# A decoder block with product-key experts: V rows beside the second search scaled by ScalarE and added by GpSimd, head norms' powers taken per projection, U tiles, rows and the spill's issue moved

## The chip, the core and the metric

The kernel runs on one core of a Trainium2 chip. The metric is the time of one execution on the device in microseconds. The engines are called by the profile's names: PE (TensorE; PEld is its weight load), DVE (VectorE), ACT (ScalarE), POOL (GpSimd) and SP (SyncE, which here only issues transfers). Each engine works through its own instructions in a fixed order; an instruction that waits holds up all those behind it on its engine.

## What is computed

One layer of a decoder block on 512 tokens of width 1024, all in f32. First come three token mixers (attention with forget gates, attention in a window, attention to 256 memory tokens) that are merged and added to x. Then comes a layer of 16384 experts, each a single neuron with a row of `u` and a row of `v`; every token picks 128 of them through two sets of 128 keys:

```python
h = rmsnorm(x, norm1_g); z = h @ w_in                    # q, k, v of the mixers, gate logits
fq = head_rmsnorm(fq, fox_q_g); fk = head_rmsnorm(fk, fox_k_g)    # likewise sq, sk, mq, mk
x += (gates0 * (o_fox @ w_fox_o) + gates1 * (o_swa @ w_swa_o) + gates2 * (o_mem @ w_mem_o)) @ w_out
h = rmsnorm(x, norm2_g); q = h @ w_q                     # 8 heads of 2 halves of 128
v1, i1 = top_k(q[..., 0] @ keys1, 16); v2, i2 = top_k(q[..., 1] @ keys2, 16)
sv, si = top_k(v1[:, None] + v2[None, :], 16)            # of 256 sums, per head
experts = i1[si // 16] * 128 + i2[si % 16]; g = softmax(sv)
x += sum_e gelu(h . u[experts_e]) * g_e * v[experts_e]   # 8 * 16 experts per token
```

## The kernel before

The 512 tokens are four blocks of 128, in two groups: block 0, and blocks 1, 2 and 3. Products of weights with activations are made of three matmuls (`mm3`, L129) from a rounded high part `whi` and the rest `wlo`: ACT rounds each loaded piece (L107), and DVE (L119) or POOL (L117) subtracts. `share[0]` says which part of the subtractions goes to POOL.

The experts are done in two ways. For blocks 0 and 1 the chosen rows of `u` and `v` are fetched one by one: a row job (`step`, L812) fetches, for one of the 128 choices, the 128 tokens' rows with one indirect transfer issued by POOL (L821, 128x1024 f32), and DVE either multiplies and sums it (a U row, L831) or adds it, scaled, to the result (a V row, L837). There are 512 such jobs in a fixed order: 128 U rows and 128 V rows of block 0, then the same of block 1. For blocks 2 and 3 all experts are computed: for each of 128 groups of experts a U tile (`dense_u`, L898: 8 matmuls of `uT` with the tokens, then a gelu on ACT, L918), and later a V tile (`dense_v`, L1027), with the gates of all experts written to DRAM in between ("spill").

Times from the trace's start, in stages:

- 0 to 198 us: mixers of block 0.
- 198 to 690 us: mixers of blocks 1 to 3 (`mixers(1, hT)`, L885). Beside them runs `beside()` (L839): first the search of block 0, then `choose`, then row jobs. `pump` (L69) hands out this side work: each load of weights adds `PACE` of the current kind to a credit, and each piece of side work takes its cost from it. Row jobs are made at a lower priority (`LATER`), so the scheduler may place them later than they stand in the program.
- 690 to 846 us: the second search (L925 to L936), for blocks 1 to 3. PE makes the scores of 8 heads (two `gemm_tr` each, L707, L711), ACT copies them out (L714), DVE finds the top 16 of each half and of the pairs (`top16`, L669), and POOL adds the pairs' sums `cand` (L686). `FIRST_U` = 8 U tiles stand in between.
- 846 to 906 us: `COVER` U tiles on PE, beside the gate weights (`weigh`, L734: three exponentials on ACT between two table loads, L741) and `choose` on DVE; then `BETWEEN` row jobs. From here on (L940) POOL, DVE and PE keep the order of the program; ACT and SP are placed by the scheduler.
- 906 to 1045 us: the spread: 64 batches of 4 tokens. DVE makes one-hot matrices (L967), POOL (odd batches, L970) or ACT (even ones, L973) scale them by the gate, PE multiplies (L985), ACT copies out (L988), and SP issues the spill every fourth batch (L991). `DURING` U tiles and 0.7 row jobs per batch stand between.
- 1045 to 1769 us: `AFTER` U tiles, then for each of 128 groups the gates are loaded back (L1006) and multiplied (L1023, L1020), and the V tile follows, with the remaining U tiles and row jobs spread evenly.

`LAG`, the U tiles that stand ahead of the first V tile, is `FIRST_U + COVER + DURING + AFTER` = 55. The tag `mm` has two PSUM banks (L61), so PE can be two U tiles ahead of ACT's gelus. Names: `tp`, `sc`, `mm`, `acc`, `tg` are PSUM banks; `two` and `raw` are loaded tiles of weights, `row` a fetched row tile, `mg` the sum x (block 0's is the first).

## Time and profile before

| | |
|---|---|
| median of 3 runs | 1769.74 us (1764.91 to 1773.3) |
| the profiled execution | 1770.86 us, of which the span of the trace is 1769.0 us |
| PE busy | 1617.1 us (91% of the span) |
| DVE, POOL, ACT busy | 1367.1, 871.8, 674.5 us (77%, 49%, 38%) |
| granted TensorE clock, mean | 0.96 |
| bytes moved | 540.16 MB, mean 305 GB/s |

PE is busy nearly throughout, but a busy share says only that an instruction is in flight, and it is a mean over stages with different limits. So the stages are read one by one; the granted clock is a share of the full 2.4 GHz, and 0.5 is the lower level of 1.2 GHz.

### The profile page before, as it was taken

What the parts mean: (1) busy time and instruction counts of PE and PEld (TensorE: products, weight loads), DVE (VectorE), ACT (ScalarE), POOL (GpSimd) and SP (SyncE); (2) the same over time, 40 slices, a digit from 0 to 9 for tenths busy, and PEclk for the clock granted to TensorE, in tenths of its full rate; (3) what the DMA queues carried; (4) which work ended last, traced back from release to release, by engine and by line L of the source; (5) the groups of instructions that cost most, each with busy time, mean ns of one, the idle gap of its engine ahead of it and who ended that gap; (6) DMA issues with size and microseconds to landing.
All of it is one profiled execution on the core that took longest, in us unless ns stands there. A gap on an engine that the chain in (4) does not pass through costs nothing.

```text
span 1769.0 us, 25245 instructions
## 1 busy us (share of the span) xinstructions
PE 1617.1 (91%) x8718; PEld 1383.7 (78%) x8718; DVE 1367.1 (77%) x2593; ACT 674.5 (38%) x1488; POOL 871.8 (49%) x728
## 2 busy tenths in 40 slices
PE   6998788998998989798799989999999999998987
PEld 6998687896987978787689978777777767776765
DVE  4777557878989999999989946766767667777767
ACT  6876555555344434221136632222222222222221
POOL 0100375546555558984058843544545445454542
PEclk8999898998998999899899999999999999999999
DMA  6887455878998998785489998999999999999986
GB/s 256 258 242 221 131 167 193 318 269 284 321 332 290 317 332 299 244 291 201 143 320 371 401 390 314 394 347 368 354 375 348 367 360 366 377 380 354 371 324 224
DMA packets 218255, 540.16 MB, mean 305 GB/s; under 512 B 18448, under 2 KB 96528, under 8 KB 218128
## 3 DMA queue, kind: packets, MB, share of 16 engines
q1 hardware_dynamic: 144400, 270.09, 43.3%
q0 software_dynamic: 73728, 268.47, 41.9%
q8 instruction: 68, 1.11, 0.3%
q14 instruction: 59, 0.48, 0.1%
HBM read 519.61 MB, written 18.87 MB: 304 GB/s over the span
## 4 chain that ended last, share of the span: by engine, by line
PE 32%; issue 31%; POOL 15%; DVE 10%; DMA 9%; ACT 3%; SPq 0%; POOLq 0%; DVEq 0%; ACTq 0%
POOL row L821 13%; PE mm L914 6%; PE mm L131 5%; PE mm L133 5%; PE mm L132 5%; DMA row<-in_peer_v_dram,eidx 5%; DVE mg L837 3%; DMA row<-in_peer_u_dram,eidx 3%; PE sc L985 1%; PE tp L985 1%; DVE wlo L119 1%; DVE tmp L673 1%; ACT whi L107 1%; PE sc L486 1%; PE tp L339 1%
## 5 line engine op out<-in xcount | busy, mean ns | idle before, releaser
L821 POOL DMA_INDIRECT row<-in_peer_u_dram,eidx x256 | 320.8, 1253 | 331.4 <-DVE scr L831 264.6
L821 POOL DMA_INDIRECT row<-in_peer_v_dram,eidx x256 | 333.9, 1304 | 281.1 <-DVE mg L837 218.5
L914 PE MATMUL mm<-h2f,two 128*128 128x256 f32 x1920 | 444.0, 383 | 16.3 <-ACT ga L918 10.1
L914 PEld LDWEIGHTS mm<-h2f,two 128*128 128x128 f32 x1920 | 364.4, 193 | 76.5 <-issue 14.6
L107 ACT CAST whi<-raw 128x1024 fp32r<-128x1024 f32 (+1 forms) x268 | 280.2, 1049 | 354.5 <-DMA raw<-in_peer_v_dram 170.5
L119 DVE TENSOR_TENSOR wlo<-raw,whi 128x1024 fp32r<-128x1024 f32 (+1 forms) x233 | 285.3, 1226 | 156.2 <-ACT whi L107 154.4
L837 DVE SCALAR_TENSOR_TENSOR mg<-row,acts,mg 128x1024 f32<-128x1024 f32 x256 | 356.6, 1393 | 19.1 <-DMA row<-in_peer_v_dram,eidx 16.1
L831 DVE SCALAR_TENSOR_TENSOR scr<-row,h2n 128x1024 bf16<-128x1024 f32 x256 | 314.0, 1227 | 19.9 <-DMA row<-in_peer_u_dram,eidx 12.9
L131 PE MATMUL mm<-whi,hhi 128*128 128x256 f32 (+1 forms) x576 | 167.1, 292 | 6.7 <-ACT hhi L623 1.9
L132 PE MATMUL mm<-wlo,hhi 128*128 128x256 f32 (+1 forms) x576 | 167.1, 291 | 2.2 <-DVE wlo L119 2.2
L133 PE MATMUL mm<-whi,hlo 128*128 128x256 f32 (+1 forms) x576 | 165.9, 290 | 1.8 <-DVE hlo L624 1.2
L918 ACT ACTIVATE ga<-mm 128x256 f32<-128x256 f32 x128 | 49.0, 385 | 285.8 <-PE mm L914 279.2
L131 PE MATMUL sc<-whi,ah 128*128 128x512 f32 x192 | 93.4, 486 | 39.8 <-ACT ah L126 39.8
L131 PE MATMUL mm<-hhi,whi 128*128 128x384 f32 x320 | 112.4, 351 | 8.8 <-ACT qp L707 5.6
L117 POOL TENSOR_TENSOR wlo<-raw,whi 128x1024 fp32r<-128x1024 f32 (+1 forms) x35 | 83.8, 2402 | 71.8 <-ACT whi L107 71.6
L131 PEld LDWEIGHTS mm<-whi,hhi 128*128 128x128 f32 x576 | 110.8, 193 | 10.1 <-ACT hhi L623 2.2
L133 PE MATMUL mm<-hhi,wlo 128*128 128x384 f32 x320 | 111.8, 349 | 4.2 <-POOL wlo L117 4.2
L132 PEld LDWEIGHTS mm<-wlo,hhi 128*128 128x128 f32 x576 | 111.3, 193 | 5.2 <-DVE wlo L119 3.1
L133 PEld LDWEIGHTS mm<-whi,hlo 128*128 128x128 f32 x576 | 110.9, 193 | 4.0 <-DVE hlo L624 1.4
L132 PE MATMUL mm<-hlo,whi 128*128 128x384 f32 x320 | 111.3, 348 | 1.5 <-DVE hlo L215 1.5
L179 POOL TENSOR_TENSOR rsy<-rsv,mhalf 128x4 f32<-128x4 f32 (+7 forms) x17 | 38.4, 2265 | 138.6 <-DVE rsv L178 138.4
L127 DVE TENSOR_TENSOR al<-gq,ah 128x256 fp32r<-128x256 f32 x96 | 40.8, 425 | 80.2 <-ACT ah L126 78.5
(260 smaller groups left out, 3020.5 us busy)
## 6 DMA issues: line engine op xcount, KB each, us to landing
raw<-in_peer_v_dram SPq DMA_DIRECT2D x128, 512.0 KB
two<-in_uT_dram SPq DMA_DIRECT2D x60, 1024.0 KB
raw<-in_w_nat_dram SPq DMA_DIRECT2D x40, 512.0 KB
gd<-st SPq DMA_DIRECT2D x32, 512.0 KB
gq<-gd SPq DMA_DIRECT2D x120, 128.0 KB
raw<-in_w_tr_dram SPq DMA_DIRECT2D x48, 256.0 KB
raw<-in_w_o_dram SPq DMA_DIRECT2D x24, 512.0 KB
raw<-in_w_tr_dram SPq DMA_DIRECT2D x24, 512.0 KB
```

Source lines behind the costliest of these rows:

```text
L107: A.copy(hi[:, :n * w], raw[:, :n * w])
L117: G.tensor_tensor(lo, raw, hi.bitcast(F32), op=OP.subtract)
L119: V.tensor_sub(lo, raw, hi.bitcast(F32))
L127: V.tensor_sub(lo, src, hi.bitcast(F32))
L131: PE.matmul(ps, lh, rh, start=first, stop=False)
L132: PE.matmul(ps, lh, rl, start=False, stop=False)
L133: PE.matmul(ps, ll, rh, start=False, stop=last)
L821: G.indirect_dma_start(out=r, out_offset=None, in_=t["peer_" + tab], in_offset=bass.IndirectOffsetOnAxis(ap=eidx[b][:, j:j + 1], axis=0))
L831: V.scalar_tensor_tensor(scr, r, 1.0, h2n[b], op0=OP.mult, op1=OP.mult, accum_out=acts[b][:, c]))
L837: V.scalar_tensor_tensor(x1[b], r, acts[b][:, c], x1[b], op0=OP.mult, op1=OP.add))
L914: PE.matmul(ps[:, :TD], w[:, dc], h2f[dc], start=dc == 0, stop=dc == KC - 1)
L918: A.activation(ga[k], ps[:, :TD], AF.Gelu)
```

## The change

It does six things. (1) During the second search a V row of block 0 is not scaled and added by one DVE instruction but scaled by ACT and added by POOL (`step(apart=True)`), a job for each 2.8 units of search cost; `beside()` ends at 176 jobs. The low parts `wlo` of that search go to DVE (`share[0]` 0.0, before 1.0). (2) The sums of pairs are made for the three blocks by one POOL instruction, right behind a head's top 16. (3) The search and `choose` of block 0 run at a higher pace, and fewer of the low parts beside them go to POOL (0.5 and 0.0, before 0.9 and 0.35). (4) The powers of the head norms, on POOL, are taken per projection, not for key and query (or two projections) together. (5) Three U tiles move from ahead of the spread into it, and two from behind it into it; the gate weights stand behind 14 covering tiles, before 5; two more row jobs stand ahead of the spread. (6) In the spread one batch in four is scaled by POOL, before one in two; the spill is issued by ACT, before by SP.

```diff
-FIRST_U, COVER, DURING, AFTER = 8, 20, 20, 7
-BETWEEN, UNWEIGHED, IN_RAW = 10, 5, 0
+FIRST_U, COVER, DURING, AFTER = 8, 17, 25, 5
+BETWEEN, UNWEIGHED, IN_RAW = 12, 14, 0
-PACE = {"search": 6.0, "choose": 4.0, "rows": 3.5}
+PACE = {"search": 9.0, "choose": 8.0, "rows": 3.5}
+EARLY_ROWS, PER_ROW = 176, 2.8
...
-    class Heads:
...
-        def scale(self):
-            r = rsqrt_mean(self.ss[:, :self.cols], self.cols, self.parts[0][3])
...
+    def heads(lhs, src, nb, nh, hd, pad=0, n=None, also=None):
...
+        ss = small_f(BIG * 4, "hss")[:, :nb * nh]
...
+        gemm_nat(lhs, src, n or nh * hd, nb, use)
+        r = rsqrt_mean(ss, nb * nh, hd)
+        for b in range(nb):
...
+            for h in range(nh):
+                A.activation(z[:, b, h, :hd], z[:, b, h, :hd], AF.Copy, scale=r[:, b * nh + h:b * nh + h + 1])
...
+        def candidates(v12):
+            cand = qq.tile([128, nb, NC], F32, tag="cand", name="cand")
+            for i0, ni, nj, c0 in ROWS:
+                G.tensor_tensor(cand[:, :, c0:c0 + ni * nj].rearrange("p b (i j) -> p b i j", j=nj),
+                                v12[:, :, 0, i0:i0 + ni, None].to_broadcast([128, nb, ni, nj]),
+                                v12[:, :, 1, None, :nj].to_broadcast([128, nb, ni, nj]), op=OP.add)
+            return cand
...
             yield from top_pairs(h - 1)
-            pairs[h] = v12
+            pairs[h] = candidates(v12)
...
-    def step():
+    def step(apart=False):
...
+        elif apart:
+            A.activation(r, r, AF.Copy, scale=acts[b][:, c])
+            G.tensor_tensor(x1[b], x1[b], r, op=OP.add)
         else:
...
-        share[0] = 0.35
+        share[0] = 0.0
...
-        while done[0] < known[0]:
+        while done[0] < EARLY_ROWS:
             step()
...
-    share[0] = 0.9
+    share[0] = 0.5
     xb, sums = mixers(1, hT)
...
-    k_u, share[0] = 0, 1.0
+    k_u, share[0] = 0, 0.0
...
         for cost in search(qq, h2T, f, BIG):
...
+            credit[0] += cost
+            while credit[0] >= PER_ROW and NJ <= done[0] < known[0]:
+                credit[0] -= PER_ROW
+                with tc.high_priority(-LATER):
+                    step(apart=True)
...
-        if n % 2:
+        if n % 4 == 3:
             G.tensor_tensor(o[:, 0], o[:, 0], eT[:, 2, ts, None].to_broadcast([128, GT, NK]), op=OP.mult)
...
-                nc.sync.dma_start(gd[i][:, t0 // TG, hf * 64 * TG:(hf + 1) * 64 * TG],
+                nc.scalar.dma_start(gd[i][:, t0 // TG, hf * 64 * TG:(hf + 1) * 64 * TG],
```

Counted in the program, the row jobs at the four milestones (end of the mixers, of the second search, of `BETWEEN`, of the spread) are 209, 209, 219 and 263 before, and 176, 210, 222 and 266 now; the U tiles at the end of the spread are 49 and 51. POOL makes 35 low parts before and 12 now.

The order of instructions at three places. The first is ACT at the end of the second search, before: the gelus of the U tiles (L918), copies of scores (L714), and the three exponentials of the gate weights (L741).

```order
L918 ACTIVATE ga<-mm 128x256
L714 COPY s<-sc 128x384 x2
L918 ACTIVATE ga<-mm 128x256 x6
L741 ACT_TABLE_LOAD
L741 ACTIVATE ex<-ex,rstd 128x128 x3
L918 ACT_TABLE_LOAD
L918 ACTIVATE ga<-mm 128x256 x17
```

The same place now, with the line numbers of the changed kernel: L819 scales a V row, L903 is the gelu, L696 the copy of scores, L723 the exponentials.

```order
L903 ACTIVATE ga<-mm 128x256
L696 COPY s<-sc 128x384
L903 ACTIVATE ga<-mm 128x256
L819 ACTIVATE row<-row,acts_174 128x1024 x2
L903 ACTIVATE ga<-mm 128x256
L819 ACTIVATE row<-row,acts_174 128x1024
L903 ACTIVATE ga<-mm 128x256
L819 ACTIVATE row<-row,acts_174 128x1024
L723 ACT_TABLE_LOAD
L723 ACTIVATE ex<-ex,rstd 128x128 x3
L903 ACT_TABLE_LOAD
```

The exponentials stand behind 8 gelus now, before behind 11; 26 of the 34 row scalings stand ahead of them on ACT, 8 behind.

The second place is POOL in the middle of the second search, before: sums of pairs (L686), low parts (L117) and the issue of V rows (L821).

```order
L686 TENSOR_TENSOR cand<-v_8697 128x24 x3
L686 TENSOR_TENSOR cand<-v_8697 128x16 x3
L821 DMA row<-in_peer_v_dram,eidx_173 128x1024
L686 TENSOR_TENSOR cand<-v_8697 128x8
L821 DMA row<-in_peer_v_dram,eidx_173 128x1024
L117 TENSOR_TENSOR wlo<-raw,whi 128x1024
L821 DMA row<-in_peer_v_dram,eidx_173 128x1024
L686 TENSOR_TENSOR cand<-v_8697 128x16
```

Now (L662 sums of pairs for three blocks, L804 the issue of a row, L820 the add of a scaled row to block 0's sum):

```order
L662 TENSOR_TENSOR cand<-v_8671 128x3x24
L662 TENSOR_TENSOR cand<-v_8671 128x3x16
L804 DMA row<-in_peer_v_dram,eidx_173 128x1024
L820 TENSOR_TENSOR mg_2214<-mg_2214,row 128x1024
L662 TENSOR_TENSOR cand<-v_8671 128x3x8
L662 TENSOR_TENSOR cand<-v_8671 128x3x16
L804 DMA row<-in_peer_v_dram,eidx_173 128x1024
L820 TENSOR_TENSOR mg_2214<-mg_2214,row 128x1024
```

The low parts have left POOL's queue here, and each issue of a row is followed by an add.

The third place is ACT in the spread, before: scalings of one-hot matrices (L973), copies out of PSUM (L988), gelus.

```order
L988 COPY st<-sc 128x64x4 x2
L918 ACTIVATE ga<-mm 128x256
L988 COPY st<-tp 128x64x4 x2
L973 ACTIVATE o<-o,eT 128x128 x4
L988 COPY st<-sc 128x64x4 x2
L918 ACTIVATE ga<-mm 128x256
L973 ACTIVATE o<-o,eT 128x128 x4
```

Now (L963 the scalings, L978 the copies, L981 the issue of the spill):

```order
L903 ACTIVATE ga<-mm 128x256
L963 ACTIVATE o<-o,eT 128x128 x4
L978 COPY st<-tp 128x64x4 x2
L963 ACTIVATE o<-o,eT 128x128 x4
L978 COPY st<-sc 128x64x4 x2
L963 ACTIVATE o<-o,eT 128x128 x4
L978 COPY st<-tp 128x64x4 x2
L981 DMA gd_9323<-st 128x1024 x2
L903 ACTIVATE ga<-mm 128x256
```

Three of four batches are scaled on ACT, and the two transfers of each spill stand in ACT's queue.

## Rows read from the trace of the kernel before

**Rows 1.** Busy time of each engine in stages of the span. Columns: the stretch in us, its length, then per engine the busy time (and the instructions), the mean granted clock as a share of full speed, the mean busy share of the 16 DMA engines, and GB/s.

```profile
198.00:293.00 95.00, 80.58 (x626) 76.01 (x626) 60.29 (x268) 50.42 (x111) 59.80 (x53) 0.98 0.55 165
690.00:846.00 156.00, 132.81 (x687) 121.98 (x685) 151.24 (x618) 34.44 (x66) 115.42 (x153) 0.93 0.70 237
846.00:906.00 60.00, 54.43 (x239) 47.20 (x240) 50.40 (x106) 9.57 (x21) 12.06 (x11) 0.91 0.57 204
906.00:1045.00 139.00, 134.74 (x873) 124.96 (x871) 129.10 (x117) 87.34 (x282) 106.44 (x78) 1.00 1.00 388
1086.00:1400.00 314.00, 298.45 (x1187) 227.66 (x1185) 220.94 (x369) 72.06 (x120) 152.94 (x114) 0.97 0.98 364
1400.00:1769.00 369.00, 337.84 (x1325) 253.90 (x1323) 264.80 (x302) 82.52 (x136) 174.12 (x125) 0.97 0.93 346
```

**Rows 2.** DVE's groups of instructions in the second search, 690 to 846 us. Columns: line, engine, operation, out<-in, shapes, count | busy us, mean ns of one | idle us before them, and what ended it.

```profile
L837 DVE SCALAR_TENSOR_TENSOR mg<-row,acts,mg 128x1024 f32<-128x1024 f32 x42 | 77.3, 1840 | 2.0 <-DMA row<-in_peer_v_dram,eidx 2.0
L673 DVE MATCH_REPLACE8 tmp<-v,s 128x128 f32<-128x128 f32 x48 | 13.6, 288 | 0.0
```

**Rows 3.** DVE's groups 597 to 690 us, same columns.

```profile
L119 DVE TENSOR_TENSOR wlo<-raw,whi 128x1024 fp32r<-128x1024 f32 x14 | 17.1, 1223 | 0.0
```

**Rows 4.** Who waited for whom, 690 to 906 us: engine and what it runs <- what ended the wait: us in total, times, the longest.

```profile
ACT s L714 <- DVE tmp L673: 26.1, 5, 10.4
ACT L741 <- DVE ex L738: 12.3, 1, 12.3
PE mm L914 <- ACT ga L918: 10.2, 2, 9.9
PE mm L131 <- ACT qp L707: 5.6, 1, 5.6
PE mm L133 <- POOL wlo L117: 4.2, 5, 1.8
```

**Rows 5.** PE in order of time around the stage of covering tiles: start, length, engine, line, operation, count [idle before <- what ended it].

```profile
829.77 11.82 PE L914 MATMUL mm<-h2f,two 128*128 128x256 f32 x54
851.46 55.05 PE L914 MATMUL mm<-h2f,two 128*128 128x256 f32 x240 [9.87 <-ACT ga L918]
906.35 0.38 PE L954 MATMUL acc<-cst,e 128*128 128x128 f32 x2
```

**Rows 6.** ACT in order of time at the same place.

```profile
847.43 1.28 ACT L741 ACT_TABLE_LOAD   x1 [12.33 <-DVE ex L738]
848.73 0.98 ACT L741 ACTIVATE ex<-ex,rstd 128x128 f32<-128x128 f32 x3
...
861.31 0.38 ACT L918 ACTIVATE ga<-mm 128x256 f32<-128x256 f32 x1 [3.07 <-PE mm L914]
864.76 0.38 ACT L918 ACTIVATE ga<-mm 128x256 f32<-128x256 f32 x1 [3.07 <-PE mm L914]
```

**Rows 7.** POOL's groups, 690 to 906 us, columns as in rows 2.

```profile
L821 POOL DMA_INDIRECT row<-in_peer_v_dram,eidx x54 | 62.2, 1152 | 67.4 <-DVE mg L837 48.5 <-issue 5.2 <-DVE tmp L673 5.1
L117 POOL TENSOR_TENSOR wlo<-raw,whi 128x1024 fp32r<-128x1024 f32 x13 | 31.2, 2397 | 0.2
L686 POOL TENSOR_TENSOR cand<-v 128x24 f32<-128x24 f32 x24 | 9.2, 401 | 8.3 <-DVE tmp L673 7.9 <-DVE best L674 0.4
```

**Rows 8.** ACT's groups, 690 to 906 us, same columns.

```profile
L107 ACT CAST whi<-raw 128x1024 fp32r<-128x1024 f32 x13 | 13.6, 1047 | 53.4 <-DMA raw<-in_w_pq_dram 32.9 <-PE mm L132 9.1 <-POOL cand L686 5.7
```

**Rows 9.** Groups of DVE, POOL and ACT in the spread, 906 to 1045 us, same columns.

```profile
L967 DVE TENSOR_TENSOR o<-tg,eT 128x1024 f32<-128x1024 f32 x64 | 76.7, 1222 | 2.6 <-PE tp L985 1.5 <-PE sc L985 0.5 <-ACT eT L956 0.4
L837 DVE SCALAR_TENSOR_TENSOR mg<-row,acts,mg 128x1024 f32<-128x1024 f32 x38 | 48.7, 1281 | 2.2 <-DMA row<-in_peer_v_dram,eidx 2.2
...
L970 POOL TENSOR_TENSOR o<-o,eT 128x512 f32<-128x512 f32 x32 | 56.3, 1758 | 18.9 <-DVE o L967 9.2 <-issue 5.2 <-ACT o L973 4.4
...
L973 ACT ACTIVATE o<-o,eT 128x128 f32<-128x128 f32 x128 | 40.9, 394 | 14.6 <-DVE o L967 14.4
```

**Rows 10.** The issue of the spill on SP: count, then the shortest, median and longest issue in ns, and the starts of the first and the last.

```profile
L991 SPq DMA_DIRECT2D gd<-st x32: 319/383/3804, 918.1 to 1044.6; - x32
```

**Rows 11.** SP in order of time at the end of the spread (columns as in rows 5).

```profile
1034.14 0.38 SPq L909 DMA_DIRECT2D two<-in_uT_dram  x1
...
1040.67 5.63 SPq L991 DMA_DIRECT2D gd<-st  x2
1046.35 6.33 SPq L1006 DMA_DIRECT2D gq<-gd  x6
```

**Rows 12.** PE and then DVE in order of time between the spread and the first V tile.

```profile
1039.65 4.05 PE L914 MATMUL mm<-h2f,two 128*128 128x256 f32 x18
1048.79 10.11 PE L914 MATMUL mm<-h2f,two 128*128 128x256 f32 x32 [5.09 <-DMA two<-in_uT_dram]
1059.96 7.14 PE L914 MATMUL mm<-h2f,two 128*128 128x256 f32 x32 [1.06 <-DMA two<-in_uT_dram]
1067.32 3.72 PE L914 MATMUL mm<-h2f,two 128*128 128x256 f32 x16 [0.21 <-ACT ga L918]
1070.69 0.58 PE L131 MATMUL sc<-whi,ah 128*128 128x512 f32 x1
...
1063.71 0.43 DVE L1023 TENSOR_TENSOR gq<-gq,ga 128x256 f32<-128x256 f32 x1 [20.74 <-PE mm L914]
```

**Rows 13.** POOL and then PE in order of time where the second mixers' first key and query heads are scaled.

```profile
282.35 9.47 POOL L179 TENSOR_TENSOR rsy<-rsv,mhalf 128x24 f32<-128x24 f32 x1 [11.09 <-DVE rsv L178]
...
292.26 0.30 PE L332 MATMUL tg<-cst,qn 128*66 128x128 f32 x1 [3.03 <-ACT qn L318]
...
298.21 0.85 PE L332 MATMUL tg<-cst,qn 128*66 128x128 f32 x3 [2.90 <-ACT kT L333]
```

**Rows 14.** POOL's groups in the second mixers, 198 to 690 us, columns as in rows 2: the powers for 24 and for 12 columns.

```profile
L179 POOL TENSOR_TENSOR rsy<-rsv,mhalf 128x24 f32<-128x24 f32 x3 | 19.3, 6438 | 11.1 <-DVE rsv L178 11.1
L179 POOL TENSOR_TENSOR rsy<-rsv,mhalf 128x12 f32<-128x12 f32 x1 | 3.2, 3207 | 0.5 <-DVE rsv L178 0.5
```

More of the change, by code (lines that the diff above doesn't have):

```diff
@@ L378, in also @@
             V.tensor_add(xf[:, bl[b]], ps[:, 256:264], b_forget)
-        heads = Heads(nb)
-        skn = heads.add(hT, t["w_skvf"], 2, 64, n=264, also=also)
-        heads.scale()
+        skn = heads(hT, t["w_skvf"], nb, 2, 64, n=264, also=also)
         tr_heads(skT[:, :, bl[0] * 128:(bl[0] + nb) * 128], skn, g_sk,
@@ L408, in memory @@
         for c in range(2):
-            heads = Heads(2)
-            kn = heads.add(mT, t["w_mem"][c], 2, 128)
-            heads.scale()
+            kn = heads(mT, t["w_mem"][c], 2, 2, 128)
             tr_heads(mkT[:, 2 * c:2 * c + 2], kn, g_mk, [lambda b, h=h: kn[:, b, h, :] for h in range(2)])
@@ L431, in fox_qkv @@
             fv[c] = pp.tile([128, NB, 256], F32, tag="v", name="v")
-        heads = Heads(nb)
-        kn = heads.add(hT, t["w_nat"][3 * c], 4, 64, pad=2)
+        kn = heads(hT, t["w_nat"][3 * c], nb, 4, 64, pad=2)
         V.memset(kn[:, :, :, 64], 1.0)
         V.tensor_scalar(kn[:, :, :, 65], cum[:, bs, hs], -1.0, None, op0=OP.mult)
-        qn = heads.add(hT, t["w_nat"][3 * c + 1], 4, 64, pad=2)
+        qn = heads(hT, t["w_nat"][3 * c + 1], nb, 4, 64, pad=2)
         V.tensor_copy(qn[:, :, :, 64], cum[:, bs, hs])
         V.memset(qn[:, :, :, 65], 1.0)
-        heads.scale()
         gemm_nat(hT, t["w_nat"][3 * c + 2], 256, nb, lambda b, ps: A.copy(fv[c][:, bl[b]], ps))
@@ L467, in window_q @@
     def window_q(g, hT):
-        qT, heads = new_q(g), Heads(len(GROUPS[g]))
-        qs = [heads.add(hT, t["w_nat"][6 + c], 4, 64) for c in range(2)]
-        heads.scale()
+        qT = new_q(g)
+        qs = [heads(hT, t["w_nat"][6 + c], len(GROUPS[g]), 4, 64) for c in range(2)]
         for c, qn in enumerate(qs):
@@ L508, in memory_q @@
     def memory_q(g, hT):
-        qT, heads = new_q(g), Heads(len(GROUPS[g]))
-        qs = [heads.add(hT, t["w_nat"][8 + c], 2, 128) for c in range(2)]
-        heads.scale()
+        qT = new_q(g)
+        qs = [heads(hT, t["w_nat"][8 + c], len(GROUPS[g]), 2, 128) for c in range(2)]
         for c, qn in enumerate(qs):
@@ L681, in top_pairs @@
                 return
-            v12 = pairs.pop(h)
-            cand = qq.tile([128, nb, NC], F32, tag="cand", name="cand")
-            for i0, ni, nj, c0 in ROWS:
-                for b in range(nb):
-                    G.tensor_tensor(cand[:, b, c0:c0 + ni * nj].rearrange("p (i j) -> p i j", j=nj),
-                                    v12[:, b, 0, i0:i0 + ni, None].to_broadcast([128, ni, nj]),
-                                    v12[:, b, 1, None, :nj].to_broadcast([128, ni, nj]), op=OP.add)
+            cand = pairs.pop(h)
             for b in range(nb):
@@ L883, in tile_block @@
     next(side[0])
-    share[0] = 0.9
+    share[0] = 0.5
     xb, sums = mixers(1, hT)
     side[0] = iter(())
-    print('ROWS', done[0])
     for lb, b in enumerate(GROUPS[1]):
```

44 lines of the change are left out of this document (15 added, 29 removed).

## The prediction

> **What bounds the kernel now.** I read the stages first [rows 1], because the page's 91% for PE is a mean. Two limits alternate. In the second search (690 to 846 us) DVE is busy 151.2 of 156 us and PE only 132.8: DVE sets the pace. 77.3 us of DVE's time there is 42 V rows, at 1840 ns each [rows 2], against 1281 ns in the spread [rows 9]; the search itself is the other 74 us. The waits say the same [rows 4]: ACT's copies of scores wait 26.1 us for DVE to free their buffers, and the exponentials 12.3 us for the search's end. That last wait reaches PE: ACT's gelus stand behind the exponentials, so PE, two U tiles ahead, stops for 9.87 us and then runs without a break to 906.35 us, where the spread begins [rows 5, 6]. From there on DVE is no longer alone. In the spread PE is busy 134.7 of 139 us, DVE 129.1, and the DMA engines are full (1.00, 388 GB/s); behind it the DMA share is 0.97 and 0.93 with PE at 95% and 92% [rows 1]. So time can be won in the search, and what is won there must pass a stage in which PE and DMA are both full.
>
> **V rows leave DVE.** DVE's work in the search becomes 151.2 - 77.3 + 13 low parts at 1.22 us [rows 3], 15.9, + 4 early V rows left on it (44 of 48 stand ahead of its first search instruction) at 1.84, 7.4: 97 us. The 34 rows cost ACT and POOL instead. No row shows either operation on these tiles. For ACT's scaling I take the cast of the same size, 1.05 us [rows 8]: 26 ahead of the exponentials are 27 us, on an engine busy 34.4 of 156 us [rows 1]. For POOL's add the nearest is the low part, 2.40 us, and the issue of a row is 1.15 [rows 7]: 3.55 us per row, 92 us for 26 rows; POOL loses 31.2 us of low parts.
>
> The sums of pairs go from 12 instructions a head to 4, each three times as wide. Small and large ones differ little, so 4 at 0.40 [rows 7] are 13 us in all, before some 34. POOL then needs about 105 us until the exponentials, and about 137 with the last eight rows. It starts near 700 us, when DVE's last early rows are in, and so ends near 840; the first DVE row that needs its sum (`BETWEEN`) comes 20 us later, behind `choose`. While that cover holds, the adds cost nothing.
>
> With DVE at 97 us PE sets the pace. Its work in the search without U tiles is 132.8 less 13 tiles (11 gelus ahead of the exponentials and two in the banks) at 3.45 us [rows 6]: 88 us. Idle that stays is 23.2 less the 4.4 of the long wait that falls into this stage and the 4.2 for POOL's low parts [rows 4]: 14.6. The last scores, behind five tiles, come at 690 + 88 + 17 + 15 = 810 us; DVE needs a head more (97/8): the search ends near 822, not 846.7. PE's tenth tile, the last before the exponentials hold it now, ends at 690 + 88 + 34.5 + 14.6 = 827. So the 9.87 us wait goes although fewer gelus stand ahead: the exponentials are ready by then. Had the search still ended at 846, the later place would cost three tiles, 10 us.
>
> The spread's start, on PE: -9.9 (that wait), -4.2 (low parts now on DVE), -10.4 (three tiles of 3.45 moved behind it), -4 (the clock stood at 0.91 in the stage after the long wait, 5.4 us of 60 [rows 1]; most of it should go with the wait), +5 for ACT's new rows ahead of copies that PE waits for (nothing if they all fit between, 27 if each delays a copy; 5.6 us of such a wait are there now [rows 4]). Sum -23.5: the spread starts near 883. DVE's own chain agrees: 24.7 us earlier, less two more `BETWEEN` rows at 1.28 (2.6), is -22. PE and DVE tie there, so neither can give more alone.
>
> **The spread gets five more U tiles**: +17.3 us if PE is the limit, +6.8 if DMA is (2.6 MB at 388 GB/s). PE's idle in it is only 4.3 us, so I take 17.3. ACT gains 64 scalings at 0.32 us (40.9/128 [rows 9]), 20.5, and 32 issues at 0.38 [rows 10], 12.3, on 87.3 us: 122 with the gelus, of about 156. That is covered as long as its waits for PE and DVE stay small. POOL loses half of its 56.3 us.
>
> **Between spread and first V tile** (1039.65 to 1070.69 us [rows 12]) two tiles go, -6.9, and PE waited 5.09 and 1.06 us for U tiles whose load stood in SP's queue with the spill [rows 11, 12]. But the first product of the gates came at 1063.7: the spill's landing and the loads back last 24 us from the last batch, of which the 5.6 us issue on SP may go. So PE, with four tiles, will wait for the gates instead. I take -7 (0 if that latency stays whole, -9 at best).
>
> **The rest.** Three row jobs fewer behind the spread, 0.52 MB each at some 355 GB/s: between 0 and -4.4, I take -2. In the second mixers PE waited 3.03 and 2.90 us for heads scaled after a power of 24 columns that lasted 9.5 us [rows 13]; 12 columns take 3.2, 24 take 6.4 on average [rows 14], and the first half now runs under the next projection: -6 at best. Against it, nine low parts go from POOL to DVE in the first 95 us, 11 us on an engine busy 60.3 [rows 1]; if they met PE's waits, +8. I take -2. The first mixers change nothing that PE waits for.
>
> **Sum:** -23.5 + 17.3 - 7 - 2 - 2 = -17.2. The span of 1769.0 becomes 1752; the profiled execution, 1770.86, becomes 1753.7. It lies 1.1 us above the median of 1769.74, so I forecast 1753 us.
>
> **Rivals.** *Nothing is left of it.* PE's work is the same in sum, and what the search saves is lost in the spread, where PE, DVE, ACT and DMA would each need 2.0 to 2.3 us per batch of 2.4. If queues that full cost 0.2 us a batch, 13 us go: 1766 us. For it speaks that the spread is at 97% on PE already; against it, that DVE's two-input work there meets half as many POOL instructions.
>
> *More comes through.* If DMA, not PE, limits everything from the spread on (1.00, then 0.97 and 0.93 [rows 1]), the bytes left at the spread's start decide: three U tiles more (1.6 MB) and three rows fewer (1.6 MB) are none, and the whole gain stays: -23.5 - 4 = 1742 us.
>
> *Slower: DVE and POOL hold each other up.* V rows on DVE take 1.84 us in the search, where POOL runs low parts, and 1.28 in the spread [rows 2, 9]: 0.56 us more. If in the same way a two-input DVE instruction (1.22 us [rows 3]) stops POOL's add once, and its issue every other time, a row costs POOL 3.55 + 1.83 = 5.4 us; 26 rows and the sums are 153 us from 700 on. ACT then stands before rows that have not landed, with the copies of scores behind them, and the search ends near 853 instead of 822; the chain behind it (62 us) puts the spread's start at 915 instead of 883, and the time is 1785 us. From (827 - 713)/26 = 4.4 us per row on it costs anything, from about 5.2 on it is slower than before. Against it: POOL's low parts took 2.40 us beside those same V rows [rows 7], so it was DVE that was held, not POOL.
>
> The Trainium skill has a rule that speaks against the change here ("SBUF — State Buffer", Who interferes with whom): DVE's second port is shared with GpSimd under an exclusive lock, and a DVE instruction with two SBUF inputs and a GpSimd instruction that reads SBUF block each other for their whole length, whichever comes second. By that rule each of the 13 low parts on DVE could wait for a whole add, 13 x 2.40 = 31 us: DVE would need 128 of the 132 us until 822 and tie with PE, which I would put at 5 us, 1758 in all. The trace bears out a part of it, 0.56 us for an instruction of 1.28, which makes 7 us on DVE and moves nothing.
>
> **How the numbers follow.** The forecast, -9 to -25, gets 0.55; nothing left 0.20; more comes through 0.12; slower 0.13. 0.5% is 8.8 us, about what a measurement here tells from no change. Faster: 0.50 of the first and 0.12 of the third, 0.62; the same: 0.05 and 0.18, 0.23; slower: 0.15. The range 1737 to 1772 leaves out the slow rival and what lies beyond the fast one; its ends take in DVE's and PE's bounds above (ACT's rows at 0 with DMA as the limit; the spread at +28).
>
> **What would show it.** Right: between 690 and about 822 us DVE falls to some 75% and PE rises above 88%; the wait of the covering tiles for a gelu is below 3 us; the spread starts near 883 and lasts about 156 us; the first V tile starts near 1055. Wrong: POOL's adds well above 2.4 us, ACT waiting for rows to land ahead of score copies, a spread of over 165 us with ACT above 90%, or a wait over 10 us at the first V tile.

## The result and the profile after

The changed kernel takes 1748.64 us in the median of 4 runs (1745.24 to 1752.0) against 1768.88 us (1764.91 to 1773.3) before: a ratio of 0.9885, 95% interval 0.9853 to 0.9916. The profiled execution took 1752.0 us, its span is 1749.9 us. The time forecast was 1753 us and the spread starts at 883.3 us, where the forecast had it near 883. The trace shows that this agreement is luck, two large errors of opposite sign. The experiments then show that the part I named wins nothing here, and that another, booked at 2 us, wins 0.9% by itself. Two single executions among the experiments below, of 8124 us (e1) and 7535 us (e6), stand outside every ratio.

Stages of the changed kernel, cut at its own events (columns as in [rows 1]): second mixers, in three parts, then the search, the way from its end to the spread, the spread, and the U tiles up to the first V tile.

```profile
198.00:293.00 95.00, 86.17 (x680) 81.97 (x680) 72.61 (x284) 60.85 (x143) 36.53 (x44) 0.98 0.53 162
293.00:590.00 297.00, 287.97 (x1815) 261.33 (x1815) 261.62 (x474) 146.66 (x357) 187.03 (x145) 0.96 0.90 315
590.00:680.00 90.00, 80.24 (x535) 77.51 (x534) 86.36 (x105) 34.56 (x66) 52.01 (x40) 0.96 0.94 337
680.00:794.00 114.00, 102.89 (x570) 96.94 (x569) 102.09 (x589) 54.84 (x79) 91.18 (x80) 0.97 0.70 234
794.00:882.00 88.00, 57.90 (x265) 49.23 (x263) 81.65 (x107) 19.91 (x32) 57.83 (x37) 0.88 0.70 239
882.00:1031.00 149.00, 147.73 (x922) 136.86 (x923) 128.16 (x118) 105.95 (x346) 75.33 (x62) 0.98 0.96 361
1031.00:1056.00 25.00, 18.42 (x76) 15.01 (x75) 1.81 (x3) 5.05 (x9) 0.00 (x0) 0.93 0.97 324
```

Against [rows 1] the search begins earlier (by its first score product 18.4 us, in the table below) and its stage lasts 114 us instead of 156: it ends at 794, not at 846. But the next stage, from the search's end to the spread, lasts 88 us instead of 60, with DVE busy 81.65 of it and PE only 57.90. PE is done with its covering tiles at 857 and stands still:

```profile
846.15 10.60 PE L899 MATMUL mm<-h2f,two 128*128 128x256 f32 x48 [0.56 <-DMA two<-in_uT_dram]
856.59 0.38 PE L944 MATMUL acc<-cst,e 128*128 128x128 f32 x2
856.80 0.27 PE L944 MATMUL acc<-cst,gate 128*128 128x128 f32 x1
883.27 2.05 PE L975 MATMUL sc<-o 128*128 128x128 f32 x8 [26.20 <-issue]
```

These are PE's rows in order of time. Before, PE ran without a break up to the same place at 906.35 [rows 5]. The 26.20 us in front of the first spread matmul (`issue`: no engine is named) end when DVE has built the first of the one-hot matrices, the sides of the product:

```profile
881.52 5.74 DVE L957 TENSOR_TENSOR o<-tg,eT 128x1024 f32<-128x1024 f32 x5
```

What DVE does ahead of it, by groups, 690 to 900 us, and then POOL:

```profile
L120 DVE TENSOR_TENSOR wlo<-raw,whi 128x1024 fp32r<-128x1024 f32 x10 | 20.2, 2018 | 2.7 <-ACT whi L108 2.7
L774 DVE TENSOR_TENSOR hot<-hot 128x1024 bf16<-128x1024 bf16 (+2 forms) x18 | 17.7, 983 | 0.6
L763 DVE CAST rb<-ri 128x128 bf16<-128x128 f32 x3 | 3.7, 1224 | 0.0
...
L820 POOL TENSOR_TENSOR mg<-mg,row 128x1024 f32<-128x1024 f32 x34 | 81.5, 2398 | 0.7
L804 POOL DMA_INDIRECT row<-in_peer_v_dram,eidx x53 | 58.6, 1106 | 41.7 <-DVE mg L823 23.4 <-POOL mg L820 5.2 <-DVE tmp L653 4.5
```

POOL's add takes 2398 ns in the mean, between 2.35 and 2.70 us, and is not slowed by much. But a low part on DVE takes 2018 ns, where [rows 3] have 1223, and the sums of one-hot products in `choose` (L774) 983 ns; the same group before:

```profile
L792 DVE TENSOR_TENSOR hot<-hot 128x1024 bf16<-128x1024 bf16 (+2 forms) x18 | 8.5, 470 | 0.6
```

In order of time one sees how. DVE in the first `choose`, and POOL in the same microseconds:

```profile
805.19 0.28 DVE L750 SCALAR_TENSOR_TENSOR p<-sh,p 128x128 f32<-128x128 uint32 x1
805.50 3.01 DVE L751 SCALAR_TENSOR_TENSOR ri<-p,p 128x128 f32<-128x128 f32 x1
808.55 0.23 DVE L753 TENSOR_SCALAR rj<-ri 128x128 f32<-128x128 f32 x1
808.69 0.22 DVE L754 TENSOR_SCALAR p<-ri 128x128 f32<-128x128 f32 x1
808.82 0.28 DVE L755 SCALAR_TENSOR_TENSOR rj<-ri,rj 128x128 f32<-128x128 f32 x1
809.14 3.01 DVE L757 SCALAR_TENSOR_TENSOR rj<-ri,rj 128x128 f32<-128x128 f32 x1
...
805.99 2.36 POOL L820 TENSOR_TENSOR mg<-mg,row 128x1024 f32<-128x1024 f32 x1
808.62 0.98 POOL L804 DMA_INDIRECT row<-in_peer_v_dram,eidx  x1 [0.27 <-POOL mg L820]
809.63 2.36 POOL L820 TENSOR_TENSOR mg<-mg,row 128x1024 f32<-128x1024 f32 x1
```

An instruction of 0.29 us takes 3.01 and ends as POOL's add ends; the next few run at once, while POOL issues a row, and the one that meets the next add stands again. DVE has about 1.3 of every 3.6 us. The first `choose` thus takes 35.2 us (801.7 to 836.9); before, the same instructions took 12.1. POOL's last add begins at 837.73, and from its end at 840 on `choose` runs as before.

### The profile page after: what moved, and what is told of

The parts are those of the page before. It is cut to its first block, busy times and chain, and to the rows that moved or that the text cites. A ratio compares the mean times of both kernels' runs of the same rounds, so it can differ in the third digit from the quotient of the medians.

```text
span 1749.9 us, 25288 instructions
## 1 busy us (share of the span) xinstructions
PE 1601.2 (91%) x8718; PEld 1373.9 (79%) x8718; DVE 1364.7 (78%) x2593; ACT 730.0 (42%) x1586; POOL 851.2 (49%) x664
## 4 chain that ended last, share of the span: by engine, by line
PE 32%; issue 29%; POOL 16%; DMA 12%; DVE 7%; ACT 3%; SPq 0%; POOLq 0%; ACTq 0%; DVEq 0%
POOL row L804 13%; PE mm L899 7%; PE mm L133 5%; PE mm L132 5%; PE mm L134 5%; DMA row<-in_peer_v_dram,eidx 5%; DMA row<-in_peer_u_dram,eidx 3%; DVE wlo L120 2%; PE sc L975 2%; POOL mg L820 2%; PE tp L975 1%; DMA two<-in_uT_dram 1%; ACT whi L108 1%; DMA raw<-in_w_pq_dram 1%; DVE mg L823 1%
## 5 line engine op out<-in xcount | busy, mean ns | idle before, releaser
L804 POOL DMA_INDIRECT row<-in_peer_u_dram,eidx x256 | 329.4, 1287 | 296.6 <-DVE scr L814 209.6
L804 POOL DMA_INDIRECT row<-in_peer_v_dram,eidx x256 | 325.5, 1272 | 276.7 <-DVE mg L823 211.0
L120 DVE TENSOR_TENSOR wlo<-raw,whi 128x1024 fp32r<-128x1024 f32 (+1 forms) x259 | 326.1, 1261 | 145.8 <-ACT whi L108 144.7
L814 DVE SCALAR_TENSOR_TENSOR scr<-row,h2n 128x1024 bf16<-128x1024 f32 x256 | 313.6, 1225 | 23.5 <-DMA row<-in_peer_u_dram,eidx 20.9
L823 DVE SCALAR_TENSOR_TENSOR mg<-row,acts,mg 128x1024 f32<-128x1024 f32 x222 | 284.5, 1282 | 10.9 <-DMA row<-in_peer_v_dram,eidx 8.0
L903 ACT ACTIVATE ga<-mm 128x256 f32<-128x256 f32 x128 | 49.0, 383 | 259.8 <-PE mm L899 255.1
L180 POOL TENSOR_TENSOR rsy<-rsv,mhalf 128x4 f32<-128x4 f32 (+5 forms) x25 | 42.6, 1705 | 145.5 <-DVE rsv L179 145.3
L127 ACT CAST ah<-gq 128x256 fp32r<-128x256 f32 x96 | 38.7, 404 | 157.5 <-DVE gq L1013 142.5
```

The lines of the kernel that those rows point to most:

```text
L120: V.tensor_sub(lo, raw, hi.bitcast(F32))
L180: G.tensor_tensor(y, v, mhalf[:, :n], op=OP.pow)
L804: G.indirect_dma_start(out=r, out_offset=None, in_=t["peer_" + tab], in_offset=bass.IndirectOffsetOnAxis(ap=eidx[b][:, j:j + 1], axis=0))
L814: V.scalar_tensor_tensor(scr, r, 1.0, h2n[b], op0=OP.mult, op1=OP.mult, accum_out=acts[b][:, c]))
L823: V.scalar_tensor_tensor(x1[b], r, acts[b][:, c], x1[b], op0=OP.mult, op1=OP.add))
L903: A.activation(ga[k], ps[:, :TD], AF.Gelu)
```

## The experiments

Times are ratios to the kernel before, run on the same chip, with 95% intervals; 0.005 is 9 us. The events are from the profiled executions, in us: first score product of the search, its end (`ex`), first spread product, first V tile, end. "Rest" is the time from the first V tile to the end.

| kernel | ratio | score | search ends | spread | V tile | end | rest |
|---|---|---|---|---|---|---|---|
| before | 1 | 693.8 | 846.7 | 909.8 | 1070.7 | 1769.0 | 698.3 |
| changed | 0.9885 [0.9853, 0.9916] | 675.4 | 794.3 | 883.3 | 1055.9 | 1749.9 | 694.0 |
| e1 rows on DVE | 0.9860 [0.9823, 0.9898] | 675.0 | 814.9 | 875.4 | 1045.3 | 1740.8 | 695.5 |
| e2 late adds out | 0.9810 [0.9782, 0.9838] | 672.9 | 789.6 | 861.3 | 1034.4 | 1728.9 | 694.5 |
| e3 24 tiles ahead | 0.9803 [0.9766, 0.9841] | 677.2 | 793.5 | 884.9 | 1039.1 | 1730.3 | 691.2 |
| e4 joint heads | 0.9929 [0.9900, 0.9958] | 698.2 | 814.6 | 889.7 | 1061.3 | 1754.8 | 693.5 |
| e5 heads alone | 0.9910 [0.9874, 0.9946] | 685.6 | 833.1 | 896.3 | 1057.8 | 1752.7 | 694.9 |
| e6 = e1 and e3 | 0.9771 [0.9728, 0.9814] | 673.1 | 814.7 | 878.6 | 1033.3 | 1727.8 | 694.5 |
| e7 low parts alone | 0.9974 [0.9946, 1.0002] | 690.1 | 832.1 | 891.5 | 1053.1 | 1763.7 | 710.6 |
| e8 rows apart alone | 0.9989 [0.9966, 1.0012] | 690.6 | 808.8 | 900.7 | 1063.2 | 1769.4 | 706.2 |
| e9 every other row | 0.9857 [0.9809, 0.9905] | 668.8 | 800.5 | 882.0 | 1038.6 | 1745.6 | 707.0 |
| e10 ACT by code | 0.9879 [0.9831, 0.9927] | 671.9 | 812.4 | 896.0 | 1053.6 | 1748.8 | 695.2 |
| e11 e7, ACT by code | 0.9952 [0.9926, 0.9978] | 696.7 | 839.1 | 898.9 | 1064.5 | 1761.1 | 696.6 |
| e12 rows end early | 0.9922 [0.9902, 0.9943] | 675.3 | 790.5 | 863.2 | 1023.4 | 1744.7 | 721.3 |

Each row of events is one execution. The changed kernel, e1, e2, e3, e6, e9, e10 and e12 differ by no edit ahead of the search, and yet their first scores lie between 668.8 and 677.2; the kernel before, e7 and e8 differ there by 3.8 us in the same way. Differences of a few us between events tell little; the ratios, from several executions each, carry the verdicts.

My theory after the two traces: the V rows taken from DVE bring the gain, and POOL's adds in `choose` take a part of it back. The rival: the gain comes from elsewhere, from the mixers above all.

**e1**, the rows back on DVE:

```diff
-                    step(apart=True)
+                    step()
```

> The changed kernel, only the V rows of the second search back on VectorE (one instruction each, none on ScalarE or GpSimd). Theory (the gain is VectorE freed of these rows; a part of it is lost again in `choose`, where GpSimd's adds hold VectorE): 34 rows at 1.84 us less 11 low parts that no add holds any more (0.7 us each) put some 50 us back on VectorE, so the search ends near 840 us instead of 794; weigh and choose then take some 60 us instead of 87, TensorE's idle ahead of the spread falls from 26 to under 5 us, the spread starts near 900 instead of 883: about 1763 us. Rival (the gain comes from the mixers' powers and from the moved tiles and spill): the spread starts where it does and the time stays within 4 us of 1749.

The time does not rise: 1744.91 us, ratio 0.9860, with an interval that overlaps that of the changed kernel. The theory's first half falls: the rows' move wins nothing in sum. The search is longer by 20.6 us, not by 46, and the way to the spread shorter by 28.5, so the spread starts 7.9 us earlier. DVE's groups, 690 to 900 us:

```profile
L823 DVE SCALAR_TENSOR_TENSOR mg<-row,acts,mg 128x1024 f32<-128x1024 f32 x52 | 66.0, 1269 | 0.8 <-DMA row<-in_peer_v_dram,eidx 0.5
L120 DVE TENSOR_TENSOR wlo<-raw,whi 128x1024 fp32r<-128x1024 f32 x9 | 10.9, 1216 | 2.0 <-ACT whi L108 2.0
L774 DVE TENSOR_TENSOR hot<-hot 128x1024 bf16<-128x1024 bf16 (+2 forms) x18 | 8.5, 470 | 0.6
```

A V row takes 1269 ns now that POOL has neither low parts nor adds; I had priced it at the 1840 of [rows 2]. Low parts and `choose` are at their old speed. But PE's wait ahead of the spread, which the theory had below 5 us, is as long as in the changed kernel:

```profile
PE sc L975 <- issue: 25.6, 1, 25.6
```

PE is done there at 849.8 and DVE begins the first sides at 873.6. So the adds in `choose` are not the only reason for that wait: with the rows on DVE the search ends later instead, PE is done 7.3 us earlier, and 17 covering tiles are too few for DVE's chain in either case.

**e2**, the adds that run behind the search left out (13 of 34; a part of the sum is missing):

```diff
+NO_ADD = 197
...
-            G.tensor_tensor(x1[b], x1[b], r, op=OP.add)
+            if n < NO_ADD:
+                G.tensor_tensor(x1[b], x1[b], r, op=OP.add)
```

> The changed kernel, the add on GpSimd left out for the last 13 rows of the second search (those that run behind its end); their loads, issues and scalings stay, so that part of the sum is missing from the output. Theory (GpSimd's adds hold the two-input instructions of `choose`): the first `choose` is back at some 0.3 us per small instruction instead of 1.2, the chain from the search's end to the last early row takes some 62 us instead of 87, TensorE's 26 us idle ahead of the spread falls below 5, the spread starts near 858: about 1730 us. Rival (the chain is longer because of the two more rows in it, the later place of the exponentials and the order of its instructions): it stays above 80 us, the idle above 20, and the time within 4 us of 1749.

The theory's second half holds: the one-hot sums are back at 470 ns, the first `choose` at 12.3 us, the way from the search's end to the spread is 71.7 us instead of 89.0, PE's long wait is gone, and the time is 1733.52. The rows' loads, issues and scalings all stay, so it is the adds that hold DVE. PE's largest waits, 680 to 910 us:

```profile
PE mm L901 <- ACT ga L905: 7.5, 3, 4.1
PE mm L901 <- DMA two<-in_uT_dram: 4.3, 2, 3.1
PE mm L133 <- ACT ga L905: 2.7, 1, 2.7
PE sc L977 <- issue: 2.3, 1, 2.3
```

**e3**, seven U tiles moved from the spread to ahead of it:

```diff
-FIRST_U, COVER, DURING, AFTER = 8, 17, 25, 5
+FIRST_U, COVER, DURING, AFTER = 8, 24, 18, 5
```

> The changed kernel with seven more U tiles ahead of the spread and seven fewer in it (COVER 24, DURING 18). Theory (TensorE's 26 us idle ahead of the spread are free room, and the spread is bound by TensorE): seven tiles at 3.45 us fill 24 us of the idle, the spread starts where it did, near 883, and falls from 150 to some 132 us, where VectorE with 128 us of work becomes its limit: about 1732 us. Rival (the DMA engines decide from the spread on, so that tiles loaded earlier give nothing): the spread stays above 145 us, and the time within 4 us of 1749.

As the theory has it: 1730.93 us. The wait at the spread is 6.4 us, the spread takes 127 us instead of 147, 20 us or 2.8 a tile. The bytes of seven tiles, 3.7 MB at 361 GB/s, would be 10 us, so it is not DMA that sets its length.

```profile
PE sc L975 <- issue: 6.4, 1, 6.4
```

**e4**, the heads as before (joint powers), all else as changed:

```diff
-        qT = new_q(g)
-        qs = [heads(hT, t["w_nat"][6 + c], len(GROUPS[g]), 4, 64) for c in range(2)]
+        qT, heads = new_q(g), Heads(len(GROUPS[g]))
+        qs = [heads.add(hT, t["w_nat"][6 + c], 4, 64) for c in range(2)]
+        heads.scale()
...
```

> The changed kernel, with the squares of two projections again put through one power of up to 24 columns, as in the kernel before. Theory (the powers of half the columns took away the two waits of 3 us and let the next projection run ahead of the scaling): the second mixers end some 8 us later, near 688 us, and everything behind them too: about 1757 us. Rival (the 10 us of the second mixers come from the pace of the side work and from low parts on VectorE): the mixers end near 680, and the time stays within 4 us of 1749.

The scores begin 22.8 us later and the search ends 20.3 later. Only 6.4 of it reach the spread, since 5 instead of 12 of POOL's adds then begin behind the search's end, and the first `choose` takes 20.2 us instead of 35.2. The ratio is 0.9929: in the changed kernel the heads are worth some 0.44%, and the two intervals still touch. PE in the second mixers:

```profile
198.00:293.00 95.00, 84.22 (x641) 78.96 (x640) 71.46 (x279) 57.13 (x135) 34.94 (x43) 0.96 0.54 165
293.00:600.00 307.00, 287.75 (x1822) 260.60 (x1822) 272.04 (x486) 150.32 (x369) 187.17 (x148) 0.95 0.89 315
```

By 590 us the changed kernel has 2495 of the second mixers' matmuls behind it (680 and 1815), this one by 600 us only 2463.

**e5**, the other way round: the kernel before with the changed heads alone.

```diff
-        heads = Heads(nb)
-        skn = heads.add(hT, t["w_skvf"], 2, 64, n=264, also=also)
-        heads.scale()
+        skn = heads(hT, t["w_skvf"], nb, 2, 64, n=264, also=also)
...
```

> The kernel before, only the heads' powers taken per projection. First theory (the mixers' end moves everything): TensorE reaches the search some 20 us earlier, near 675 us, and the time falls as much, to about 1748 us. Second theory (VectorE is full of V rows from 590 us on and does not care when TensorE comes): the search's end moves by less than half of that, and the time is about 1758 us.

The ratio is 0.9910, some 16 us, where the whole change gives 20. Without the heads it gives some 13 (e4), so the parts do not add up to the whole. Neither theory has the way: the scores begin 8.2 us earlier (not 20), the search ends 13.6 earlier, the spread starts 13.5 earlier, and the rest keeps it. Counted by matmuls, PE is 5.7 us ahead of the kernel before at its 1300th, near 200 us, and 11.8 ahead at its 2500th, near 380. The first 95 us of the second mixers, 85.13 us busy against 80.58 [rows 1], are a part of it:

```profile
198.00:293.00 95.00, 85.13 (x679) 80.62 (x678) 60.45 (x272) 60.41 (x144) 56.35 (x56) 1.00 0.55 167
```

**e6**, e1 and e3 together.

```diff
-FIRST_U, COVER, DURING, AFTER = 8, 17, 25, 5
+FIRST_U, COVER, DURING, AFTER = 8, 24, 18, 5
...
-                    step(apart=True)
+                    step()
```

> The changed kernel with the V rows of the search back on VectorE and with 24 U tiles ahead of the spread (the edits of the two runs with these names together). Theory (the spread starts when VectorE's chain ends, near 875 us with the rows on VectorE and 883 with them on GpSimd, and the tiles moved ahead fill TensorE's idle time): the spread starts near 876, lasts some 130 us, and the time is about 1724 us. Rival (the DMA engines give the same time whenever the tiles are loaded by then): 1731 us, as with the rows on GpSimd.

1729.58 us, ratio 0.9771: faster than the kernel before and than the changed one, without the V rows apart. Its spread starts 6.3 us before that of e3, but the intervals of the two overlap, so which of them is better is not settled.

**e7**, the kernel before with the low parts of the search on DVE.

```diff
-    k_u, share[0] = 0, 1.0
+    k_u, share[0] = 0, 0.0
```

> The kernel before, only the low parts of the second search on VectorE instead of GpSimd. Theory (GpSimd's low parts hold the V rows): a V row in the search takes 1.27 us instead of 1.84, 24 us less over 42 rows, against 13 low parts at 1.22 us, 16 us: the search ends some 8 us earlier and the time is about 1759 us. Rival (V rows are slow there for another reason, such as the DMA writes of the rows beside them): they stay at 1.8 us, the search ends 16 us later, about 1780 us.

The mechanism is right. DVE's groups while both run, 705 to 790 us:

```profile
L837 DVE SCALAR_TENSOR_TENSOR mg<-row,acts,mg 128x1024 f32<-128x1024 f32 x34 | 43.7, 1285 | 0.9 <-DMA row<-in_peer_v_dram,eidx 0.6 <-issue 0.2
L119 DVE TENSOR_TENSOR wlo<-raw,whi 128x1024 fp32r<-128x1024 f32 x9 | 11.0, 1227 | 1.3 <-ACT whi L107 0.6 <-issue 0.6
```

1285 ns instead of 1840, the search ends 14.6 us earlier and the first V tile starts 17.6 earlier (3.7 of each are there at the first score, ahead of the edit). Yet the time is within the error of before: the rest took 710.6 us instead of 698.3.

**e8**, the kernel before with the V rows of the search on ACT and POOL and its low parts on DVE, which is the first part of the change.

```diff
+        elif apart:
+            A.activation(r, r, AF.Copy, scale=acts[b][:, c])
+            G.tensor_tensor(x1[b], x1[b], r, op=OP.add)
...
-    k_u, share[0] = 0, 1.0
+    k_u, share[0] = 0, 0.0
...
+            while credit[0] >= PER_ROW and NJ <= done[0] < known[0]:
+                credit[0] -= PER_ROW
+                with tc.high_priority(-LATER):
+                    step(apart=True)
```

> The kernel before, only the V rows in the second search scaled by ScalarE and added by GpSimd, with the low parts there on VectorE (both of the changed kernel's numbers for it kept: 176 early rows, 2.8 per row). Theory (VectorE's search falls to some 107 us; GpSimd is done with its 34 adds near 812 us, before `choose`): the search ends near 812, `choose` runs at its old 41 us, TensorE with 20 covering tiles reaches the spread near 890 instead of 910: about 1750 us. Rival (as in the changed kernel, GpSimd's adds stand in `choose` and give back what the search saves): the chain from the search's end to the spread stays above 75 us, and the time is above 1760 us.

No gain: 0.9989. The search ends at 808.8, as the theory has it, but the way to the spread takes 91.9 us, as the rival has it, because POOL's 34 adds end at 862, not 812. `choose` is slow in another group, 809 to 900 us:

```profile
L793 DVE TENSOR_TENSOR hot<-hot 128x1024 bf16<-128x1024 bf16 (+2 forms) x18 | 13.1, 728 | 0.6
L790 DVE TENSOR_TENSOR hot<-hot,idb 128x2048 bf16<-128x2048 bf16 x6 | 11.4, 1906 | 0.2
```

**e9**, half of the rows apart, so that POOL is done in time, and five U tiles moved ahead of the spread.

```diff
-FIRST_U, COVER, DURING, AFTER = 8, 17, 25, 5
+FIRST_U, COVER, DURING, AFTER = 8, 22, 20, 5
...
-                    step(apart=True)
+                    step(apart=done[0] % 2 == 0)
```

> The changed kernel with only every other V row of the search on ScalarE and GpSimd, the others on VectorE, and 22 U tiles ahead of the spread (DURING 20). Theory (GpSimd's adds cost only where they run beside the two-input instructions of weigh and `choose`, and 17 of them at 3.6 us are done by 760 us, ahead of these): the search ends near 800 us, weigh and `choose` take their old 41 us, the spread starts near 862, and the time is about 1726 us, some 4 us less than with all rows on VectorE and 24 tiles ahead. Rival (GpSimd's adds hold the search's low parts and V rows as much as they relieve VectorE, wherever they stand): the search ends near 815, the spread starts at 876 or later, and the time is above 1732 us.

The search ends at 800, as in the theory, and the first `choose` takes 17.0 us, still more than the 12.1 of before, since two adds begin behind the search's end and the last ends at 814. PE arrives only at 880 (12.6 us of waits for gelus, ACT's L903), and the rest takes 707.0 us. The ratio of 0.9857 is not better than e1's.

**e10** and **e11**, ACT's instructions from the covering tiles on in the order of the code, on e6 and on e7. The rest of e7 had not only been longer; the scheduler had also written ACT's casts, splits and gelus there in another order than before.

```diff
-    ctx.enter_context(tc.manual_schedule(engines={mybir.EngineType.Pool, mybir.EngineType.DVE, mybir.EngineType.PE}))
+    ctx.enter_context(tc.manual_schedule(engines={mybir.EngineType.Pool, mybir.EngineType.DVE, mybir.EngineType.PE, mybir.EngineType.Activation}))
```

> The changed kernel with V rows on VectorE and 24 U tiles ahead of the spread, and ScalarE's instructions from the covering tiles on in the order of the code, as VectorE's, GpSimd's and TensorE's are, instead of in the scheduler's. Theory (the order of ScalarE's casts, splits and gelus beside the V tiles costs TensorE waits for `ah`, some 40 us there): the last stage shrinks from 694 to some 685 us: about 1720 us. Rival (these waits end with the V tile's load, whatever the order): the last stage stays within 4 us of 694 and the time near 1729; if a gelu that waits for TensorE now stands ahead of a split, it is longer.

> The kernel before, with the low parts of the search on VectorE and ScalarE's instructions from the covering tiles on in the order of the code. With the low parts alone the first V tile came 17.6 us earlier, but the last stage took 710.6 us instead of 698.3, and ScalarE's order there was another than before. Theory (that order took 12 us back): in the order of the code the last stage takes at most 698 us again and the time is about 1752 us. Rival (the DMA engines took it back): it stays near 710, the time near 1766.

e10 loses 20 us against e6 ahead of the first V tile, 17.4 of them ahead of the spread: its exponentials now stand behind the gelus, and the first `choose` ends at 852 instead of 831. Its rest, 695.2 us, is that of e6 (694.5), so the order is worth nothing there. In e11 the rest is 696.6 instead of 710.6, as its theory has it, but its first V tile comes 11.4 us later than that of e7: 6.6 us are there at the first score, ahead of what the edit touches, and 4.4 come between the end of the spread and the V tile. The two do not agree on the cause, and e9 has a long rest in an order much like that of e1, which has a short one. It is not the clock: 0.97 is granted there in e7 and e9 as in the kernel before. PE idles 55.7 and 53.4 us in these two, 42.6 before. What lengthens the rest of e7, e8 and e9 by 8 to 13 us stays open.

**e12**, 21 rows apart instead of 34, the other 13 later, and three U tiles moved ahead of the spread; nothing is left out.

```diff
-FIRST_U, COVER, DURING, AFTER = 8, 17, 25, 5
+FIRST_U, COVER, DURING, AFTER = 8, 20, 22, 5
...
-EARLY_ROWS, PER_ROW = 176, 2.8
+EARLY_ROWS, PER_ROW, LAST_APART = 176, 2.8, 197
...
-            while credit[0] >= PER_ROW and NJ <= done[0] < known[0]:
+            while credit[0] >= PER_ROW and NJ <= done[0] < LAST_APART:
```

> The changed kernel with only the first 21 V rows of the search on ScalarE and GpSimd (so that none is left behind the search's end), the other 13 done later, beside the V tiles, and 20 U tiles ahead of the spread (DURING 22). Nothing is left out. With the last 13 adds left out `choose` was at its old speed and the spread started at 861 us; TensorE with three more tiles ahead comes at some 868, and the first V tile near 1030. Then 13 rows of 0.52 MB more, 6.8 MB, have to pass the last stage. Theory (the last stage is bound by TensorE, which waits there some 40 us for the splits anyway): it stays near 694 us, and the time is about 1726 us. Rival (the DMA engines, 0.96 busy there, bound it): 6.8 MB at some 355 GB/s add 19 us to it, and the time is about 1745 us, where the changed kernel is.

The first V tile starts at 1023.4, 32.5 us before that of the changed kernel, and 27.3 of these are lost in the rest: 0.9922. The rival decides, with more than its price (2.1 us a row, against 1.5 by bytes); whether the 8 us beyond it are the rows' or the open lengthening of e7, e8 and e9 is not shown. PE's waits there, first of e12 and then of the changed kernel:

```profile
PE sc L132 <- ACT ah L127: 59.5, 30, 6.1
```

```profile
PE sc L132 <- ACT ah L127: 41.1, 24, 4.6
```

So these 13 rows, moved behind the first V tile, are paid there in full. What is done earlier by the same instructions was kept in e3 and e6, and not in e9.

## Why the prediction came out as it did

The number was right; the mechanism it rested on, DVE freed of its V rows, was not what brought it. By steps:

- **The second mixers** were mis-sized. I took -2 us, "-6 at best", from the two waits at the first heads [rows 13]. Those two waits are gone, but the scores begin 18.4 us earlier. The heads give 8.2 us of that alone (e5), and taking them out of the changed kernel costs 22.8 (e4). There PE idles 42.2 us between 198 us and the scores, against 27.5 in the changed kernel; the largest wait that went, 6.6 us at 436 us (3.9 in the kernel before), is for DVE at an attention's output, far behind the heads. I counted the waits in one place; waits further on went as well, and which of them follow from the heads is not shown. Part of the lead, 5.7 us in e5, is there near 200 us, where I had the first mixers change nothing that PE waits for. Heads alone are worth 0.9% (e5), the whole change 1.15%.
- **The search** was mis-sized by more. I had it end at 822 us, bound by PE; it ended at 794.3. 18.4 us of the 52.4 are the mixers'. From the first score on it takes 118.9 us instead of 152.9, 34 less, where I had 22 to 25. Of these 34, 21 are the rows (e1: 139.9 us), and the other 13 are there in e1 too, with the rows on DVE; the low parts' move alone makes the search 10.9 us shorter (e7: 142.0).
- **What a V row costs** was priced at 1.84 us as if it were the row's own. It was POOL's low parts that made it so: e7 takes only those away, and a row takes 1.285 us. I had the two numbers side by side in the slow rival, and used them to price POOL instead of DVE.
- **The low parts on DVE** were priced at 1.22 us and took 2.02: 8 us for ten, near the 7 that I took from the V rows (and, by the trace, a third of a whole add each). That one held.
- **"While that cover holds, the adds cost nothing"** is the step that failed outright. POOL's row took 3.6 us and its last add ended at 840, as forecast (the 137 us there should read 134). By the forecast's own times, 822 and 840, five adds already ran behind the search's end. It ended 28 us earlier than that, so 12 ran beside weigh and `choose`. I looked only at who waits for the sum, not at what the adds do to DVE. Price: 26 us on the way from the search's end to the spread, 2.6 of them for the two more rows there. e2 gives 17 of it back, and then PE is what comes last: it waits 2.3 us there, as the 3.0 before.
- **"PE and DVE tie"** was wrong: PE was done at 857.1, and DVE began the sides at 881.5; with the rows on DVE (e1) these are 849.8 and 873.6. PE was not last, so the -10.4 for three U tiles moved into the spread bought nothing at its start, and the spread paid for them. With 24 tiles ahead of it 0.8% more is won (e3).
- **The spread's start**: by its first product I had 909.8 - 23.5 - 2 = 884.3, and 883.3 was measured. But it is -18.4 (mixers), -34.0 (search) and +25.9 (the way to the spread), where I had -2, some -25 and next to nothing. Of the marks I had set, PE above 88% in the search (90%), its waits for gelus below 3 us (2.8 the longest) and the spread's start came true, and DVE at 75% did not (90%).
- **The spread** took 147.0 us instead of 130.0 by its first and last product: +17.0 for +17.3. **Behind it** 25.6 us instead of 30.9, -5.3 for -7: the first product of the gates came 24.7 us after the last batch (23.9 before), so the spill's new queue won nothing there, and PE still waited 5.24 us for a U tile. **The rest** was 4.3 us shorter for -2.
- **Not taken apart:** the sums of pairs, the pace, the spread's scalings and the spill's issue were never run alone. The rows with the low parts alone win nothing (e8), the heads alone 16 us of the 20 (e5); which parts make up the remainder stays open.

Of the rivals, the slow one had the right two engines and the wrong victim: POOL's adds were not held (2.40 us in the mean), DVE was. The Trainium skill's rule ("SBUF — State Buffer", Who interferes with whom), that a DVE instruction with two SBUF inputs and a GpSimd instruction that reads SBUF block each other for their whole length, speaks of this place too. The trace agrees with it in `choose`, 3.01 us for 0.29 beside an add of 2.36, where I had applied it to the low parts only; that the adds were blocked in their turn it does not show (2.35 to 2.70 us). The fast rival, that DMA limits from the spread on, is borne out in the stage of the V tiles by e12, and not in the spread (e3).

## What to carry to other kernels

When work is moved to GpSimd to free VectorE, list the VectorE instructions that will run beside it, two-input ones above all (a cast was held here too), in the stage where it really ends and not only in the one it was meant for, and give each up to the length of a whole GpSimd instruction. A forecast time that comes true proves no step of it: here the named cause won nothing, neither undone (e1) nor alone (e8), while a part booked at 2 us won 0.9% by itself (e5). When a stage begins earlier by another engine's chain, look at what the other engines do in the gap: filling PE's 26 us with U tiles (e3) was worth another 0.8%.
